# Searching the top-k thresholds of a hybrid decoder block: four of seven query blocks on ScalarE with 16-bit integer keys, three on VectorE

## The chip, the cores and the metric

The program runs on one core of one Trainium2 chip. The metric is the device time of one execution in microseconds (us); of several runs the median is taken. The engines go by the names of the profile: PE is TensorE's matrix product (PEld its weight load), DVE is VectorE, ACT is ScalarE, POOL is GpSimd, SP is SyncE, which issues most transfers. Each engine works through its own queue strictly in order, and waits for others by semaphores.

## The reference

A decoder block for 1024 tokens behind 16 meta tokens. Two attentions run on the same normed input: a sliding window with sinks, and a sparse attention whose keys an indexer chooses. Only the indexer's choice matters here:

```python
score = jnp.einsum('bqhs,bqh->bqs', jax.nn.relu(logits).astype(jnp.float32), wi.astype(jnp.float32))
admissible = (kpos[None, :] <= qpos[:, None]) & (kpos[None, :] >= PAD)
score = jnp.where(admissible[None], score, -jnp.inf)
_, sel = lax.top_k(score, topk)          # topk = 256 of up to 1040 keys
valid = (sel <= qpos[None, :, None]) & (sel >= PAD)
```

Each query keeps its 256 best keys, the earlier key first where scores are equal, and the sparse attention is a softmax over those alone. Behind the two attentions come gates, the output projection and a SwiGLU.

## The kernel before, in words

The tokens lie in eight blocks of 128 queries. Block j sees `width(j)` = 16 + 128(j+1) keys (144 for block 0, 1040 for block 7). Block 0 needs no choice; for blocks 1 to 7 the kernel finds, for each of the 128 queries of a block (one per partition), the exact 32-bit threshold that 256 scores reach, and turns it into an additive mask of 0 and -1e30 (`self.mask[j]`).

The search (`select_topk`) is by bits. The upper 16 bits of the scores lie as bf16 in `self.high[j]`. For each of 16 bits `count` compares all keys of a block with the trial threshold and adds up the hits in the same instruction (L772, one instruction for each block, and a short one that reads the accumulator); two small steps on [128 x 7] numbers set or clear the bit for all seven blocks at once (L779, L780). One more count closes the upper half. Then POOL takes the lower 16 bits of the scores (L789), DVE keeps those whose upper half equals the threshold's (L790), and 16 more bits are counted in them, with three small steps each (L794 to L796). At the end the mask is built: compare with the full threshold (L772 again, L808), a running count of equal scores for the ties (L809, a scan), two combinations (L810, L811), the scale to 0 and -1e30 (L812), and the causal edge (POOL, L534).

What runs beside the search: `proj_tokens`, `window_inputs`, `latents` and `sparse_inputs` project the tokens on PE (L189); ACT takes the products out of PSUM (L561 to L564, L601, L603) and rounds the weights to a high part (L183), POOL computes the low part (L184). `latents` needs DVE in the middle of it: L215 to L220 compute a reciprocal square root in some twelve small steps (`rlat`), L582 scales the rows by it (`lraw`), PE transposes them (L194), ACT and DVE split them into `ck` and `qn` (L125, L131). Then comes the window attention (`window_setup`, 16 calls of `window_block`): a DVE clear (L147) of the values `va`, the keys `ka` (load, ACT L685, DVE L686), products `s<-ka` (L189), a DVE step (L718) on each, and so on. Products of the gates (`gps`, `gt`, `w_hi`, `w_lo`; L835, L836) are spread between all this by a list of marks, so that PE has something to do.

What sets the order: the framework schedules every engine's queue ahead of time with a timeline of its own, and where two instructions could both go, the one that was written first goes first. `select_topk` is written ahead of `proj_tokens` and all that follows, so on DVE the steps of the search go first, and other work enters where the search has to wait for a result of its own.

Of the kernel before, what the change touches and what calls it, by code (L numbers as in the profile page):

```python
# [18 lines left out]
P = 128  # L19
# [3 lines left out]
NB = T // P  # L23
# [49 lines left out]
def width(j):  # L73
    return NM + P * (j + 1)
# [25 lines left out]
class Program:  # L100
# [18 lines left out]
    def split(self, ps, hi, lo, scale=None, lo_pool=False):  # L119
# [4 lines left out]
        else:  # L124
            nc.scalar.activation(hi, ps, AF.Copy, scale=scale)  # L125
        if lo_pool:
# [6 lines left out]
    def spread(self, ps, hi, lo, scale):  # L133
# [5 lines left out]
        for e in range(2):  # L139
            own, other = slice(64 * e, 64 * e + 64), slice(64 - 64 * e, 128 - 64 * e)  # L140
            nc.scalar.activation(hv[own, :, e, :], ps[own], AF.Copy, scale=scale)
            nc.vector.scalar_tensor_tensor(lv[:64, :, e, :], ps[own], scale, hv[own, :, e, :].bitcast(F32),
# [309 lines left out]
    def indexer(self, ip):  # L452
# [56 lines left out]
        for j in range(1, NB):  # L509
            W = width(j)  # L510
            iqt = iqts[j]
# [245 lines left out]

    def select_topk(self, ap):

        nc = self.nc  # L760
        n = NB - 1
        nc.vector.memset(self.mask[0], 0.0)
        self.causal(self.mask[0][:, NM:], P, 0, NEG)
        small = ap.tile([P, 7 * n], F32, name="small")
        cnt, thr, d, need, low, sign, base = [small[:, n * i:n * i + n] for i in range(7)]
        tb, d = thr.bitcast(I32), d.bitcast(I32)
        nc.vector.memset(thr, 0.0)
        rows = range(1, NB)

        def count(op, at, src, out=cnt):  # L770
            for j in rows:
                nc.vector.tensor_scalar(self.mask[j], src[j], at[:, j - 1:j], None, op0=op, op1=ALU.add, accum_out=out[:, j - 1:j])  # L772

        for k in range(31, 15, -1):
            count(ALU.is_ge, thr, self.high)
            nc.vector.tensor_scalar(d, cnt, float(TOPK), -65536.0 if k == 31 else float(1 << k), op0=ALU.is_lt, op1=ALU.mult)  # L779
            nc.vector.scalar_tensor_tensor(tb, d, 1 << (k - 1) if k > 16 else 0, tb, op0=ALU.bitwise_xor, op1=ALU.bitwise_xor)  # L780
        nc.vector.tensor_scalar(base, tb, 0.0, 65535.0, op0=ALU.is_lt, op1=ALU.mult)
        nc.vector.tensor_scalar(sign, base, -2.0 / 65535, 1.0, op0=ALU.mult, op1=ALU.add)
        count(ALU.is_gt, thr, self.high, need)
        nc.vector.tensor_scalar(need, need, -1.0, float(TOPK), op0=ALU.mult, op1=ALU.add)
        lows = [None] + [h.bitcast(U16) for h in self.high[1:]]
        for j in rows:
            half = self.mask[j].bitcast(U16)
            src = self.scores[j].bitcast(U16).rearrange("p (n e) -> p n e", e=2)[:, :, 0]
            nc.gpsimd.tensor_scalar(half, src, sign[:, j - 1:j], base[:, j - 1:j], op0=ALU.mult, op1=ALU.add)  # L789
            nc.vector.scalar_tensor_tensor(lows[j], self.high[j], thr[:, j - 1:j], half, op0=ALU.is_equal, op1=ALU.mult)  # L790
        nc.vector.memset(low, 32768.0)
        for k in range(15, -1, -1):
            count(ALU.is_ge, low, lows)
            nc.vector.tensor_sub(cnt, cnt, need)  # L794
            nc.vector.tensor_scalar(cnt, cnt, 0.0, 0.5 if k else 1.0, op0=ALU.is_ge, op1=ALU.subtract)
            nc.vector.scalar_tensor_tensor(low, cnt, float(1 << k), low, op0=ALU.mult, op1=ALU.add)  # L796
        nc.vector.tensor_mul(low, low, sign)
        nc.vector.tensor_add(d, low, base)
        nc.vector.scalar_tensor_tensor(tb, d, 0, tb, op0=ALU.bitwise_xor, op1=ALU.bitwise_xor)
        count(ALU.is_gt, thr, self.scores)  # L800
        nc.vector.tensor_scalar(cnt, cnt, -1.0, float(TOPK), op0=ALU.mult, op1=ALU.add)
        for j in rows:
            W = width(j)
            s = self.scores[j]
            t = thr[:, j - 1:j]
            eq = self.mask[j]
            rank = self.high[j].bitcast(mybir.dt.int16)
            nc.vector.tensor_scalar(eq[:, :W], s, t, None, op0=ALU.is_equal)  # L808
            nc.vector.tensor_tensor_scan(rank[:, :W], eq[:, :W], eq[:, :W], 0.0, op0=ALU.add, op1=ALU.max)  # L809
            nc.vector.scalar_tensor_tensor(eq[:, :W], rank[:, :W], cnt[:, j - 1:j], eq[:, :W], op0=ALU.is_le, op1=ALU.mult)  # L810
            nc.vector.scalar_tensor_tensor(eq[:, :W], s, t, eq[:, :W], op0=ALU.is_gt, op1=ALU.add)  # L811
            nc.vector.tensor_scalar(self.mask[j], eq[:, :W], -1.0, -NEG, op0=ALU.add, op1=ALU.mult)  # L812
            self.causal(self.mask[j][:, W - P:], P, 0, NEG)

    def gates(self, *cuts):
        behind, n, marks = list(self.tensor_insts), (32 - LATE) * KC * 3, [None] * GSP[0]
# [654 lines left out]
```

## Time and profile before

| | |
|---|---|
| median of 3 runs | 1561.67 us (1555.85 to 1562.71) |
| the profiled execution, device time | 1559.75 us |
| its span, first to last instruction | 1558.0 us |
| PE busy | 1394.5 us (90% of the span) |
| DVE busy | 1132.3 us (73%) |
| ACT busy | 709.2 us (46%) |
| POOL busy | 822.9 us (53%) |
| mean granted TensorE clock | 0.957 of full speed |

The profiled execution lies 1.9 us under the median. Its span leaves 1.75 us of the device time outside. Busy shares are averages over stages that have different limits; which wait counts has to be read stage by stage. Durations of single instructions overlap a little at their ends, so where many follow each other the distance from start to start is the price.

### The profile page before, as it was taken

The page shows a single profiled execution, that of the slowest core. Times are in us where ns is not written, and L with a number is a line of the kernel's source. Part 1 is how long each engine was busy: PE and PEld are TensorE (multiplying, and loading weights), DVE is VectorE, ACT ScalarE, POOL GpSimd, SP SyncE. Part 2 cuts the span into 40 slices and gives each one's busy share as a digit, 9 for nine tenths or more (in the row PEclk, how much of TensorE's full clock was granted, in tenths as well). Part 3 has the DMA queues.
Part 4 walks back from the last instruction along what each step waited for, and adds up shares of the span by engine and source line. Part 5 has one row for each costly group of instructions (what it writes and reads, how often), then busy time and mean ns, then how long its engine had stood idle before and what let it go on. Part 6 is the DMA issues. An engine that isn't in the chain of part 4 may idle for free.

```text
span 1558.0 us, 21095 instructions
## 1 busy us (share of the span) xinstructions
PE 1394.5 (90%) x6847; PEld 1155.7 (74%) x6847; DVE 1132.3 (73%) x2205; ACT 709.2 (46%) x1479; POOL 822.9 (53%) x768
## 2 busy tenths in 40 slices
PE   4999966295699899999999789999999999999997
PEld 4989955184577687889777568888888888878876
DVE  6268999999877678778498995444444446698576
ACT  5344311142288677777334553333333334433463
POOL 4232304113566555675588385555555557596575
PEclk9999998697899899999999899999999999999999
DMA  6420212044333755434861113332333338822332
GB/s 201 129 75 28 77 53 68 28 162 124 106 108 102 186 129 171 146 112 144 277 222 54 54 34 116 108 108 102 103 103 103 104 104 289 324 75 95 119 119 108
DMA packets 148036, 189.77 MB, mean 122 GB/s; under 512 B 11331, under 2 KB 95126, under 8 KB 147670
## 3 DMA queue, kind: packets, MB, share of 16 engines
q1 hardware_dynamic: 147568, 188.28, 37.5%
q8 instruction: 54, 0.88, 0.2%
q14 instruction: 56, 0.46, 0.1%
q10 hardware_dynamic: 198, 0.14, 0.0%
q0 software_dynamic: 160, 0.01, 0.0%
HBM read 133.49 MB, written 58.03 MB: 123 GB/s over the span
## 4 chain that ended last, share of the span: by engine, by line
PE 56%; DVE 27%; DMA 6%; POOL 4%; issue 4%; ACT 2%; SPq 1%; POOLq 0%; DVEq 0%; ACTq 0%
PE ps L189 22%; PE s L189 17%; DVE mask L772 12%; PE gps L189 8%; PE pv L970 2%; PE s L928 2%; PE tp L959 1%; DMA kraw<-bk_dram 1%; PE tp L194 1%; PE pv L189 1%; POOL yhl L1353 1%; POOL y L1432 1%; DVE high L809 1%; DVE fhl L1353 1%; DMA wd<-in_w_ffn_down 1%
## 5 line engine op out<-in xcount | busy, mean ns | idle before, releaser
L1282 POOL TENSOR_TENSOR fhl<-fs,fhl 128x512 fp32r<-128x512 f32 x88 | 121.3, 1400 | 99.1 <-ACT fhl L1281 99.1
L772 DVE TENSOR_SCALAR_CACHE_REDUCE mask<-high,small 128x272 bf16<-128x272 bf16 (+9 forms) x165 | 153.3, 972 | 3.6 <-POOL high L529 2.6
L1282 POOL TENSOR_TENSOR fhl<-fr,fhl 128x512 fp32r<-128x512 f32 x66 | 105.2, 1614 | 84.7 <-ACT fhl L1281 72.9
L184 POOL TENSOR_TENSOR w_lo<-w_raw,w_hi 128x512 fp32r<-128x512 f32 x60 | 82.4, 1375 | 114.3 <-ACT w_hi L183 99.8
L189 PE MATMUL s<-ht,fhl 128*128 128x512 f32 x384 | 123.3, 396 | 2.4 <-ACT fhl L1281 2.0
L1353 POOL TENSOR_TENSOR yhl<-wd,yhl 128x512 fp32r<-128x512 f32 x66 | 96.1, 1461 | 54.4 <-ACT yhl L1352 54.3
L1353 DVE TENSOR_TENSOR fhl<-da,fhl 128x512 fp32r<-128x512 f32 x66 | 89.4, 1369 | 46.4 <-ACT fhl L1352 46.3
L189 PE MATMUL ps<-ht,fhl 128*128 128x512 f32 x320 | 101.1, 392 | 0.0
L189 PE MATMUL gps<-oh,w_hi 128*128 128x512 f32 x232 | 96.0, 414 | 4.6 <-ACT gt L835 4.5
L189 PE MATMUL s<-yhl,fhl 128*128 128x512 f32 x396 | 92.4, 391 | 2.5 <-POOL yhl L1353 2.3
L189 PE MATMUL gps<-ol,w_hi 128*128 128x512 f32 x232 | 94.0, 405 | 0.0
L189 PE MATMUL gps<-oh,w_lo 128*128 128x512 f32 x232 | 93.5, 403 | 0.0
L189 PE MATMUL ps<-yhl,fhl 128*128 128x512 f32 x396 | 92.1, 391 | 1.5 <-DVE fhl L1353 1.5
L189 PEld LDWEIGHTS s<-yhl,fhl 128*128 128x128 f32 x396 | 73.9, 188 | 20.2 <-POOL yhl L1353 4.3
L189 PE MATMUL s<-h,fhl 128*128 128x512 f32 x272 | 88.7, 397 | 0.0
L189 PEld LDWEIGHTS ps<-yhl,fhl 128*128 128x128 f32 x396 | 73.9, 188 | 18.9 <-DVE fhl L1353 3.1
L189 PEld LDWEIGHTS s<-ht,fhl 128*128 128x128 f32 x384 | 72.8, 190 | 20.0 <-ACT fhl L1281 2.9
L129 DVE TENSOR_TENSOR ptl<-tp,pth 128x512 fp32r<-128x512 f32 (+2 forms) x112 | 70.8, 646 | 22.7 <-ACT pth L123 22.3
L189 PE MATMUL ps<-h,fhl 128*128 128x512 f32 x256 | 82.4, 393 | 3.6 <-ACT h L1239 3.6
L1352 ACT CAST yhl<-wd 128x512 fp32r<-128x512 f32 x66 | 40.9, 620 | 94.6 <-PE ps L189 42.8
L189 PE MATMUL s<-lt,fhl 128*128 128x512 f32 x192 | 76.0, 396 | 1.6 <-DVE lt L1240 1.6
L1281 ACT CAST fhl<-fr 128x512 fp32r<-128x512 f32 x66 | 39.7, 619 | 74.4 <-issue 33.2
(456 smaller groups left out, 4245.7 us busy)
## 6 DMA issues: line engine op xcount, KB each, us to landing
fr<-in_w_ffn_gate SPq DMA_DIRECT2D x22, 512.0 KB, 3.8
fr<-in_w_ffn_up SPq DMA_DIRECT2D x22, 512.0 KB, 4.7
wd<-in_w_ffn_down SPq DMA_DIRECT2D x44, 256.0 KB, 5.3
da<-acts SPq DMA_DIRECT2D x44, 256.0 KB, 3.8
w_raw<-in_w_in SPq DMA_DIRECT2D x40, 256.0 KB, 3.2
act<-a SPq DMA_DIRECT2D x33, 256.0 KB, 2.0
da<-act SPq DMA_DIRECT2D x33, 256.0 KB, 3.0
acts<-s SPq DMA_DIRECT2D x33, 256.0 KB, 2.0
```

The costliest lines, as they stand in the source:

```text
L129: nc.vector.tensor_sub(lo, ps, hi.bitcast(F32))
L184: (nc.vector if lo_dve else nc.gpsimd).tensor_sub(t[1], t[2], t[0].bitcast(F32))
L189: mm = self.nc.tensor.matmul(*args, **kw)
L194: mm = self.nc.tensor.transpose(*args)
L772: nc.vector.tensor_scalar(self.mask[j], src[j], at[:, j - 1:j], None, op0=op, op1=ALU.add, accum_out=out[:, j - 1:j])
L809: nc.vector.tensor_tensor_scan(rank[:, :W], eq[:, :W], eq[:, :W], 0.0, op0=ALU.add, op1=ALU.max)
L928: nc.tensor.matmul(ps[:, :n], q[k][:, h, qc:qc + P], kb[:, h, at:at + n], start=k == 0, stop=k == 1)
L970: mm = nc.tensor.matmul(acc[:, e, :], v, t[k][:, 256 * i:256 * i + 256], start=r + i + k == 0, stop=False)
L1281: nc.scalar.copy(hi, a[name])
L1282: nc.gpsimd.tensor_sub(lo, a[name], hi.bitcast(F32))
L1352: nc.scalar.copy(hi, src)
L1353: (nc.gpsimd if pool else nc.vector).tensor_sub(lo, src, hi.bitcast(F32))
```

## The change

`DVE_ROWS = (6, 4, 1)` stay with VectorE and the algorithm of before (`search_dve`; the small steps now work on [128 x 3]). `ACT_ROWS = ((7, 2), (5, 3))` are two groups that ScalarE searches (`search_act`). Their upper halves become signed 16-bit integer keys (POOL L849, DVE L851). A trial is one ACTIVATE of Sign over all keys of a block with a bias for each query and the sum of the signs in the accumulator (L857); POOL compares the sum for each block (L865) and makes the next bias for the group (L866). 16 bits on the keys, one closing count, the low halves (POOL and DVE, `low_halves`), 16 bits on those, and six small DVE steps that put the threshold together. The three searches are written as generators and called in turn, a bit each. The masks are built as before, except that the scale to 0 and -1e30 moves from DVE to POOL.

The diff, cut:

```diff
+DVE_ROWS = (6, 4, 1)
+ACT_ROWS = ((7, 2), (5, 3))
...
+        searches = [self.search_act(ap, f"g{i}", g, thr[:, places[g[0]]:places[g[0]] + len(g)]) for i, g in enumerate(ACT_ROWS)]
+        searches.append(self.search_dve(ap, DVE_ROWS, thr[:, :nd]))
+        while searches:
+            searches = [s for s in searches if next(s, None) is not None]
+        for j in range(1, NB):
+            nc.vector.tensor_scalar(self.mask[j], self.scores[j], col(thr, j), None, op0=ALU.is_gt, op1=ALU.add, accum_out=col(cnt, j))
...
-            nc.vector.tensor_scalar(self.mask[j], eq[:, :W], -1.0, -NEG, op0=ALU.add, op1=ALU.mult)
+            nc.gpsimd.tensor_scalar(self.mask[j], eq[:, :W], -1.0, -NEG, op0=ALU.add, op1=ALU.mult)
...
+    def low_halves(self, j, equal, sign, base):
...
+        nc.gpsimd.tensor_scalar(half, src, sign, base, op0=ALU.mult, op1=ALU.add)
+        nc.vector.scalar_tensor_tensor(self.lows[j], *equal, half, op0=ALU.is_equal, op1=ALU.mult)
...
+    def search_act(self, ap, tag, rows, thr):
...
+        for i, j in enumerate(rows):
+            key, t = keys[j], t = self.high[j].bitcast(I16), self.mask[j].bitcast(I16)
+            g.tensor_scalar(t, key, 0.0, 32767.0, op0=ALU.is_lt, op1=ALU.mult)
+            k32 = key.bitcast(I32)
+            nc.vector.tensor_tensor(k32, k32, t.bitcast(I32), op=ALU.bitwise_xor)
...
+        def count(src, at, out, scale=1.0):
+            for i, j in enumerate(rows):
+                nc.scalar.activation(self.mask[j], src[j], AF.Sign, bias=at[:, i:i + 1], scale=scale, accum_out=out[:, i:i + 1])
...
+            for k in range(15, -1, -1):
+                count(src, b, acc, 2.0 ** -k)
+                for i in range(n):
+                    o = slice(i, i + 1)
+                    g.tensor_scalar(c[:, o], acc[:, o], bar[:, o], b[:, o], op0=ALU.is_ge, op1=ALU.subtract)
+                g.tensor_scalar(b, c, -2.0 if k else -1.0, 1.0, op0=ALU.mult, op1=ALU.add)
+                yield k
...
+        nc.vector.tensor_add(l, T1, base)
+        nc.vector.tensor_scalar(h, T0, 1.0, 0.0, op0=ALU.mult, op1=ALU.add)
+        nc.vector.tensor_scalar(t, T0, 0.0, 32767.0, op0=ALU.is_lt, op1=ALU.mult)
+        nc.vector.tensor_tensor(h, h, t, op=ALU.bitwise_xor)
+        nc.vector.tensor_scalar(h, h, 16, None, op0=ALU.logical_shift_left)
+        nc.vector.tensor_tensor(thr.bitcast(I32), h, l, op=ALU.bitwise_or)
```

In the changed kernel all later lines have other numbers: L561 of before is L565, L582 is L586, L147 is L151, L183 and L184 are L187 and L188, L685 and L686 are L689 and L690, L718 is L722, L835 is L914. The numbers of PE's products do not change, 6847 in all, but their order does.

The first place is ACT's queue while the second part of `proj_tokens` is taken out of PSUM (`junk`, `lraw`, `vraw` are the three readings of one product). Before:

```order
L561 ACTIVATE junk,ssq<-ps 128x128
L562 COPY lraw<-ps 128x128
L564 COPY vraw<-ps 128x128
L561 ACTIVATE junk,ssq<-s 128x128
L562 COPY lraw<-s 128x128
L564 COPY vraw<-s 128x128
```

In the changed kernel, same place (`mask_151` and `mask_146` are blocks 7 and 2, `mask_149` and `mask_147` blocks 5 and 3):

```order
L565 ACTIVATE junk,ssq<-s 128x128
L566 COPY lraw<-s 128x128
L568 COPY vraw<-s 128x128
L857 ACTIVATE mask_149,smallg_1221<-high,smallg_1221 128x784
L857 ACTIVATE mask_147,smallg_1221<-sc_203,smallg_1221 128x528
L565 ACTIVATE junk,ssq<-ps 128x128
L566 COPY lraw<-ps 128x128
L568 COPY vraw<-ps 128x128
```

One group's pass, two ACTIVATEs, now stands between two readings of products.

POOL's queue at the same place in the changed kernel (before, POOL had the weights' low parts and the gates alone there):

```order
L865 TENSOR_SCALAR smallg_1221<-smallg_1221 128x1 x2
L866 TENSOR_SCALAR smallg_1221<-smallg_1221 128x2
L188 TENSOR_TENSOR w_lo<-w_raw,w_hi 128x512
L865 TENSOR_SCALAR smallg_1208<-smallg_1208 128x1 x2
L866 TENSOR_SCALAR smallg_1208<-smallg_1208 128x2
L915 TENSOR_SCALAR gt<-gt 128x512
```

The three small steps behind each pass share the queue with the weights' low parts and the gates.

The second place is DVE's queue where `lraw` is scaled. Before, just behind the closing count of the upper half (17 of 33 counts are done):

```order
L782 TENSOR_SCALAR small_1206<-small_1206 128x7
L772 TENSOR_SCALAR mask4_148,small_1206<-high_204,small_1206 128x656
L772 TENSOR_SCALAR mask5_149,small_1206<-high_204,small_1206 128x784
L772 TENSOR_SCALAR mask6_150,small_1206<-high_204,small_1206 128x912
L772 TENSOR_SCALAR mask7_151,small_1206<-high_204,small_1206 128x1040
L582 TENSOR_SCALAR lraw_1607<-lraw_1607,rlat_y_2119 16x128
```

In the changed kernel, behind the last bit of DVE's own search:

```order
L833 TENSOR_SCALAR smalld_1234<-smalld_1234 128x3
L223 SCALAR_TENSOR_TENSOR rlat_a_2359<-rlat_a_2359,ssq_1849 128x18
L834 SCALAR_TENSOR_TENSOR smalld_1234<-smalld_1234 128x3
L224 SCALAR_TENSOR_TENSOR rlat_y_2358<-rlat_a_2359,rlat_y_2358 128x18
L836 TENSOR_TENSOR smalld_1234<-smalld_1234 128x3
L586 TENSOR_SCALAR lraw_1846<-lraw_1846,rlat_y_2358 16x128
```

`lraw` moved from the middle of the search of seven blocks to the end of the search of three.

The third place is the end of the masks and the start of the window attention on DVE. Before, the clears stood between the scans:

```order
L809 SCALAR_TENSOR_TENSOR high_204<-mask4_148 128x656
L147 CAST va_2831<-zero_284 128x256
L151 CAST qlo0_2852<-zero_284 64x1024
L151 CAST qlo1_2853<-zero_284 64x1024
L147 CAST pth_2900<-zero_284 128x512
L147 CAST ptl_2901<-zero_284 128x512
L809 SCALAR_TENSOR_TENSOR high_204<-mask5_149 128x784
```

In the changed kernel they stand behind the last mask step:

```order
L791 SCALAR_TENSOR_TENSOR mask2_146<-sc1_203,small_1206,mask2_146 128x400
L791 SCALAR_TENSOR_TENSOR mask7_151<-sc0_202,small_1206,mask7_151 128x1040
L151 CAST va_3070<-zero_284 128x256
L155 CAST qlo0_3091<-zero_284 64x1024
L155 CAST qlo1_3092<-zero_284 64x1024
L151 CAST pth_3139<-zero_284 128x512
L151 CAST ptl_3140<-zero_284 128x512
L690 TENSOR_TENSOR ka0_3079<-kraw_3081,ka0_3079 64x1040
```

The clear of `va`, which starts the loads of the window attention's keys, now waits for the masks of blocks 7 and 2.

## Rows read from the trace of the kernel before

**Rows 1.** Busy time by stage. Columns: the stretch in us from the span's start, its length, then busy us and count of PE, PEld, DVE, ACT, POOL, then the granted TensorE clock, the share of the DMA engines and GB/s.

```profile
137.00:222.00 85.00, 84.98 (x589) 78.13 (x588) 83.17 (x211) 23.59 (x80) 15.34 (x13) 1.00 0.21 60
222.00:244.00 22.00, 0.00 (x0) 0.00 (x0) 22.00 (x64) 0.00 (x0) 4.90 (x7) 0.62 0.00 0
244.00:274.60 30.60, 28.59 (x117) 21.83 (x117) 30.36 (x69) 7.70 (x15) 14.36 (x9) 0.94 0.29 95
274.60:304.10 29.50, 0.07 (x2) 0.02 (x1) 28.95 (x76) 1.12 (x3) 3.07 (x3) 0.56 0.07 18
304.10:366.00 61.90, 61.90 (x277) 51.23 (x278) 60.73 (x159) 22.59 (x42) 10.17 (x10) 0.96 0.53 172
366.00:421.00 55.00, 28.09 (x104) 21.86 (x104) 52.52 (x63) 10.30 (x14) 24.91 (x20) 0.75 0.27 74
421.00:539.00 118.00, 103.64 (x535) 83.54 (x534) 84.94 (x257) 90.79 (x247) 72.17 (x102) 0.97 0.45 125
```

**Rows 2.** Who PE waited for between 137 and 430 us: us in total, times, the longest.

```profile
PE tp L194 <- DVE qn L131: 29.4, 1, 29.4
PE tp L194 <- DVE lraw L582: 22.2, 1, 22.2
PE s L189 <- DVE ka L686: 10.9, 1, 10.9
```

**Rows 3.** DVE in order of time, one bit of the upper half (start us, us): counts of some of the seven blocks (272 keys are block 1, 400 block 2, 784 block 5, 912 block 6, 1040 block 7), and the next bit's first count.

```profile
139.36 0.50 DVE L772 TENSOR_SCALAR_CACHE_REDUCE mask<-high,small 128x272 bf16<-128x272 bf16 x1
139.78 0.63 DVE L772 TENSOR_SCALAR_CACHE_REDUCE mask<-sc,small 128x400 bf16<-128x400 bf16 x1
...
141.02 0.89 DVE L772 TENSOR_SCALAR_CACHE_REDUCE mask<-high,small 128x656 bf16<-128x656 bf16 x1
...
141.84 1.02 DVE L772 TENSOR_SCALAR_CACHE_REDUCE mask<-high,small 128x784 bf16<-128x784 bf16 x1
...
142.79 1.16 DVE L772 TENSOR_SCALAR_CACHE_REDUCE mask<-high,small 128x912 bf16<-128x912 bf16 x1
...
143.87 1.29 DVE L772 TENSOR_SCALAR_CACHE_REDUCE mask<-high,small 128x1040 bf16<-128x1040 bf16 x1
...
145.62 0.50 DVE L772 TENSOR_SCALAR_CACHE_REDUCE mask<-high,small 128x272 bf16<-128x272 bf16 x1
```

**Rows 4.** DVE in order of time: the first small step of two lower bits that follow each other.

```profile
264.35 0.17 DVE L794 TENSOR_TENSOR small<-small 128x7 f32<-128x7 f32 x1
...
270.82 0.16 DVE L794 TENSOR_TENSOR small<-small 128x7 f32<-128x7 f32 x1
```

**Rows 5.** DVE in order of time: where block 7's scores begin, the two small steps of one bit while POOL computed low parts of weights, and the scaling of `lraw` (ten instructions).

```profile
129.83 0.97 DVE L524 TENSOR_SCALAR sc<-relu,iw 128x1040 f32<-128x1040 f32 x1 [0.98 <-ACT relu L520]
...
157.71 1.04 DVE L779 TENSOR_SCALAR small<-small 128x7 int32<-128x7 f32 x1
158.78 1.22 DVE L780 SCALAR_TENSOR_TENSOR small<-small 128x7 int32<-128x7 int32 x1
...
242.95 5.20 DVE L582 TENSOR_SCALAR lraw<-lraw,rlat_y 16x128 f32<-16x128 f32 x10
```

**Rows 6.** PE in order of time: two products of 512 columns that follow each other.

```profile
215.64 0.39 PE L189 MATMUL s<-oh,wa_hi 128*128 128x512 f32 x1
215.86 0.39 PE L189 MATMUL s<-ol,wa_hi 128*128 128x512 f32 x1
```

**Rows 7.** ACT by line and shape: busy us, mean ns of one. An Exp over the keys of a block with a bias for each query and a sum in the accumulator, late in the kernel.

```profile
L935 ACT ACTIVATE pb<-pb,st 128x1040 f32<-128x1040 f32 x8 | 9.4, 1172 | 3.3 <-DVE st L932 3.3
L935 ACT ACTIVATE pb<-pb,st 128x784 f32<-128x784 f32 x8 | 7.6, 955 | 1.6 <-DVE st L932 1.4
L935 ACT ACTIVATE pb<-pb,st 128x528 f32<-128x528 f32 x8 | 5.9, 739 | 0.3 <-DVE st L932 0.3
L935 ACT ACTIVATE pb<-pb,st 128x400 f32<-128x400 f32 x8 | 5.1, 634 | 0.9 <-DVE st L932 0.9
```

**Rows 8.** POOL's smallest arithmetic step, from the listing of one source line: ns (min/median/max), first and last start, shape.

```profile
L936 POOL TENSOR_SCALAR pmq<-pb x64: 196/203/1167, 543.2 to 727.3; 128x16 f32<-128x16 f32 x64
```

**Rows 9.** POOL by line and shape (busy us, mean ns): low parts of the weights.

```profile
L184 POOL TENSOR_TENSOR wa_lo<-wa_raw,wa_hi 128x512 fp32r<-128x512 f32 x22 | 31.5, 1440 | 69.8 <-ACT wa_hi L183 69.6
```

**Rows 10.** The chain that ended last, in order of time, at the end of the masks (start us, us).

```profile
370.82 5.80 DVE mask L772 x14
...
391.02 10.06 DVE high L809 x3
401.08 5.87 DVE mask L810 x7
...
408.02 4.55 DVE mask L811 x6
412.57 0.03 issue
412.60 1.25 DVE ka L686
413.85 0.04 issue
413.89 1.13 PE s L189 x4
```

**Rows 11.** ACT in order of time: its part of the window attention's first keys, with the wait ahead of it.

```profile
390.19 1.06 ACT L685 CAST ka<-kraw 128x1040 fp32r<-128x1040 f32 x1 [2.43 <-DMA kraw<-wk_dram]
```

More of the change, by code (lines that the diff above doesn't have):

```diff
@@ L12 @@
 U16 = mybir.dt.uint16
+I16 = mybir.dt.int16
 AF = mybir.ActivationFunctionType
@@ L763, in select_topk @@
         self.causal(self.mask[0][:, NM:], P, 0, NEG)
-        small = ap.tile([P, 7 * n], F32, name="small")
-        cnt, thr, d, need, low, sign, base = [small[:, n * i:n * i + n] for i in range(7)]
+        small = ap.tile([P, 2 * n], F32, name="small")
+        thr, cnt = small[:, :n], small[:, n:]
+        nc.vector.memset(thr, 0.0)
+        self.lows = [None] + [h.bitcast(U16) for h in self.high[1:]]
+        places = {j: i for i, j in enumerate((*DVE_ROWS, *[j for g in ACT_ROWS for j in g]))}
@@ new lines, in select_topk @@
+        col = lambda t, j: t[:, places[j]:places[j] + 1]
+        nd = len(DVE_ROWS)
+        searches = [self.search_act(ap, f"g{i}", g, thr[:, places[g[0]]:places[g[0]] + len(g)]) for i, g in enumerate(ACT_ROWS)]
[4 more added lines that the diff above has]
+            nc.vector.tensor_scalar(self.mask[j], self.scores[j], col(thr, j), None, op0=ALU.is_gt, op1=ALU.add, accum_out=col(cnt, j))
@@ new lines, in select_topk @@
+        nc.vector.tensor_scalar(cnt, cnt, -1.0, float(TOPK), op0=ALU.mult, op1=ALU.add)
+        for j in range(1, NB):
+            W = width(j)
+            s, t = self.scores[j], col(thr, j)
+            eq = self.mask[j]
+            rank = self.high[j].bitcast(I16)
+            nc.vector.tensor_scalar(eq[:, :W], s, t, None, op0=ALU.is_equal)
+            nc.vector.tensor_tensor_scan(rank[:, :W], eq[:, :W], eq[:, :W], 0.0, op0=ALU.add, op1=ALU.max)
+            nc.vector.scalar_tensor_tensor(eq[:, :W], rank[:, :W], col(cnt, j), eq[:, :W], op0=ALU.is_le, op1=ALU.mult)
+            nc.vector.scalar_tensor_tensor(eq[:, :W], s, t, eq[:, :W], op0=ALU.is_gt, op1=ALU.add)
+            nc.gpsimd.tensor_scalar(self.mask[j], eq[:, :W], -1.0, -NEG, op0=ALU.add, op1=ALU.mult)
+            self.causal(self.mask[j][:, W - P:], P, 0, NEG)
@@ new lines, in low_halves, with search_dve @@
+    def low_halves(self, j, equal, sign, base):
+        nc = self.nc
+        half = self.mask[j].bitcast(U16)
+        src = self.scores[j].bitcast(U16).rearrange("p (n e) -> p n e", e=2)[:, :, 0]
+        nc.gpsimd.tensor_scalar(half, src, sign, base, op0=ALU.mult, op1=ALU.add)
+        nc.vector.scalar_tensor_tensor(self.lows[j], *equal, half, op0=ALU.is_equal, op1=ALU.mult)
+    def search_dve(self, ap, rows, thr):
+        nc, n = self.nc, len(rows)
+        small = ap.tile([P, 6 * n], F32, name="smalld")
+        cnt, d, need, low, sign, base = [small[:, n * i:n * i + n] for i in range(6)]
@@ L766, in select_topk @@
         tb, d = thr.bitcast(I32), d.bitcast(I32)
-        nc.vector.memset(thr, 0.0)
-        rows = range(1, NB)
         def count(op, at, src, out=cnt):
-            for j in rows:
-                nc.vector.tensor_scalar(self.mask[j], src[j], at[:, j - 1:j], None, op0=op, op1=ALU.add, accum_out=out[:, j - 1:j])
+            for i, j in enumerate(rows):
+                nc.vector.tensor_scalar(self.mask[j], src[j], at[:, i:i + 1], None, op0=op, op1=ALU.add, accum_out=out[:, i:i + 1])
         for k in range(31, 15, -1):
@@ L784, in select_topk @@
         nc.vector.tensor_scalar(need, need, -1.0, float(TOPK), op0=ALU.mult, op1=ALU.add)
[L785 to L790, printed above, removed]
+        for i, j in enumerate(rows):
+            c = slice(i, i + 1)
+            self.low_halves(j, (self.high[j], thr[:, c]), sign[:, c], base[:, c])
         nc.vector.memset(low, 32768.0)
         for k in range(15, -1, -1):
-            count(ALU.is_ge, low, lows)
+            count(ALU.is_ge, low, self.lows)
             nc.vector.tensor_sub(cnt, cnt, need)
@@ L796, in select_topk @@
             nc.vector.scalar_tensor_tensor(low, cnt, float(1 << k), low, op0=ALU.mult, op1=ALU.add)
+            yield k
         nc.vector.tensor_mul(low, low, sign)
```

39 lines of the change are left out of this document (26 added, 13 removed).

## The prediction

> **What bounds the kernel now.** I read the busy times by stage first. Over the whole span PE is busy 90%, but in three stages it is not: 222 to 244 us, 274.6 to 304.1 and 366 to 421. There it is busy 0, 0.07 and 28.09 us, while DVE is full (22.00 of 22, 28.95 of 29.5, 52.52 of 55), and the granted clock is 0.62, 0.56 and 0.75 [rows 1]. Then I read whom PE waited for: 22.2 us for `lraw`, 29.4 for `qn`, 10.9 for the first `ka`, all three written by DVE [rows 2]. So from 130 to 414 us the search on DVE sets the time, and the projections of PE lie beside it, cut in pieces by single DVE steps that queue behind the search. The profiled execution (1559.75 us, 1.9 under the median) is my base. What counts is when the first product of the window attention starts, 413.89 us before: behind it stands the same work in nearly the same order, so I take a shift of that start as the shift of the end.
>
> **DVE's own search.** One bit of the upper half takes 6.26 us from start to start for seven blocks; of it block 1 takes 0.42, block 4 0.82 and block 6 1.08, and what no count holds is the 0.53 us between the end of block 7's count and the next bit (145.62 − 143.87 − 1.22, its slot) [rows 3]. Three blocks: 2.32 + 0.53 = 2.85 us a bit. A lower bit takes 6.47 us, 0.2 more, since it has one small step more [rows 4]: 3.04 with three blocks. From 129.8 us, where block 7's scores begin and take 5.2 us [rows 5]: 5.2, the rest of the first pass 1.6, 15 × 2.85 = 42.8, the flips of the integer keys 1.1, the closing count with base and sign 2.9, low halves 4 (an estimate, from three counts and a hand-over to POOL), 16 × 3.04 = 48.6, and some 2.8 for steps of the other searches and of `rlat`. That is 109 us, so `lraw` could be scaled at 239.
>
> DVE's small steps are dearer while POOL works: 1.04 and 1.22 us where the same kind takes 0.17 [rows 4, 5]. Now POOL has more to do, and DVE more small steps for each us. About ten of 32 bits met such a step before; at 0.9 us each I add 8 us. `lraw` at **247 us**, against 242.95 before [rows 5]: scarcely moved, though it now stands behind a whole search. PE gets to this wait earlier: 47 products fewer stand ahead of it, and two of 512 columns start 0.22 to 0.23 us apart [rows 6], so 10.7 of the 85 us [rows 1] go, and some 3 come from waits for ACT, whose passes stand between the readings of PSUM. PE is there at 213 to 217 and waits some 30 us (22.2 before).
>
> **PE from `lraw` to the first `ka`.** Nothing of the search on DVE is left there, so the wait for `qn` (29.4) goes, and the 47 products plus 22 from later stages, 69 in all, fill in. The path: before, PE was busy 28.59 + 61.90 + some 21 (of the 28.09 us of the last stage, what lay ahead of 413.89) = 111.6 us [rows 1]. Plus 69 × 0.228 = 15.7: 127 us at the clocks of before. At full clock the same 478 products and the small ones come to 117. That puts PE at the first `ka` between 247 + 117 = 364 and 374. I take 372, since a gap of 30 us stands ahead of it, and behind such gaps the stretch was granted 0.94 to 0.96, not 1 [rows 1].
>
> **ACT's search.** No row shows a Sign. The nearest is Exp with a bias for each query and a sum in the accumulator: 1172 ns for 1040 keys, 634 for 400, 955 for 784, 739 for 528 [rows 7]. From start to start I take 0.01 less: a pass of blocks 7 and 2 costs 1.78 us, one of 5 and 3 1.68. Bounds: DVE's own count of 1040 keys (1.29 us) above [rows 3], and half of Exp's price below; the Exp is nearest, being the same instruction with another function. One pass of each group hides what POOL does for the other: two steps of [128 x 1] and one of [128 x 2], at 0.2 us (POOL's smallest arithmetic step: median 203 ns, worst 1167) [rows 8], 0.6 us behind a pass of 1.7. What isn't hidden is when a low part of a weight, 1440 ns on POOL [rows 9], stands ahead. POOL is then taken about a third of the time; I take 0.3 us for each pass.
>
> ACT's order puts one eviction (`ck`, which needs PE's transposes of `lraw`) ahead of 14 passes of one group and 18 of the other, so until 248 us ACT can do the first halves only, and the rest comes after: 14 × 1.68 + 18 × 1.78 = 55.5 us, plus some 20 of evictions and roundings of weights (two thirds of the 7.70 + 1.12 + 22.59 us that ACT had from 244 to 366 [rows 1]), plus 32 × 0.3 = 10 us of hand-over: the searches end near **334 us**. Behind that come on DVE six small steps (2 us), the counts and compares of the last two blocks (3, of the 5.80 for seven [rows 10]), their scans (4 to 6; three long ones took 10.06), and seven and seven combinations (5.87, and 4.55 for six plus 1.3): 21 us in all, 355. The clear of `va` now comes behind these masks; it starts the loads of the keys, and from the clear to ACT's copy of the first `ka` lie 0.3 on DVE, 0.9 on ACT and POOL and 4.9 for the load, then 1.06 on ACT [rows 11] and 1.25 on DVE [rows 10]: 8.4 us, which before lay beside the scans. First product at 363.5 by this path.
>
> The scale of the masks leaves DVE and goes to POOL, some 2.5 us less on DVE and 6 more on POOL; the causal edge on POOL that follows it is not waited for until the sparse attention, so I put it at nothing. If that cover were gone, it would cost these 6 us.
>
> **The sum.** The later of the two paths: 372 (PE), 363.5 (ACT). 413.89 − 372 = 42 us: 1559.75 − 42 = **1518 us**, with 1502 to 1538 for PE at full clock with no waits (356) up to an exposure of 1.1 us a pass (392).
>
> **The rule that speaks against this.** ACT's Exp takes 1172 ns for 1040 keys, DVE's count 1.29 us for the same keys [rows 3, 7]: the two engines stand level. The Trainium skill ("ScalarE: Activation LUTs", section "Rules for kernel authors") says to keep simple arithmetic off ScalarE, since VectorE is up to about 3 times faster for each element in bf16 with one source. By that rule a pass of both groups would be 11.1 us (3 × the counts of 1.29, 1.02, 0.76 and 0.63) and not 3.5; the searches would end 110 us later. The rows bear it out only for plain copies; a count with a sum is not such.
>
> **The rivals.**
>
> *POOL's answer is exposed, break-even.* The chain of one group is pass, wait, three POOL steps, wait, pass. If the exposure is x us a pass and not 0.3, the first product comes at 352.5 + 32x, and at x = 1.92 at 413.89: no gain (1557). For it: the queue of POOL holds 1440 ns steps [rows 9]; against: these have gaps of their own, and the other group covers 1.7 us.
>
> *The same mechanism, slower than before.* Place: POOL between two passes on ACT. Price: three steps at 1167 ns (the worst of the small ones [rows 8]), which happen when DVE works beside it, plus 0.4 behind a low part, less what is covered: x = 3.6. First product at 468, 1559.75 + 54 = **1613**. It decides from x = 1.92 on. For it: POOL and DVE lengthen each other's steps [rows 5]; against: the median is 203 ns [rows 8].
>
> *DVE's small steps wait for POOL in every bit.* 1.9 us (1.04 + 1.22 less two of 0.17 [rows 4, 5]) × 32 = 61: `lraw` at 300 and the first product at 417 to 427: 1563 to 1573. For it: POOL has three more steps for every pass; against: those are short.
>
> *Better than forecast.* No exposure, full clock: 239 + 117 = 356, and 22 products fewer (5 us) behind it: 1497.
>
> *ACT at a third of DVE's pace:* first product at 473, 1619 us. It is what the rule of the Trainium skill cited above would make; the trace speaks against it (1172 ns against 1.29 us).
>
> **How the numbers follow.** Forecast 0.66; better 0.09; break-even 0.10; slower through POOL 0.08; DVE behind POOL 0.06; ACT slow 0.01. About half of the break-even case would still show a gain over 0.5% (7.8 us, about what a measurement of this kernel can tell from no change), and half of the DVE case would be a loss over it. Faster: 0.66 + 0.09 + 0.05 = 0.80; same: 0.05 + 0.03 = 0.08; slower: 0.08 + 0.03 + 0.01 = 0.12. The range goes from 1492, a little under the better case, to 1555, where the break-even case begins; it leaves out about 2 in 10.
>
> **What would show it.** `lraw` scaled near 247 us with some 30 us of idle PE ahead of it and a low clock there; no wait for `qn`; ACT's Sign at 1.17 us for 1040 keys, the last one near 334; POOL's three steps at 0.2 us each, with a wait of ACT for POOL of some 10 us in all; the first product of the window attention near 372. I am wrong on DVE if `lraw` is later than 260, on ACT if the last Sign comes after 345, and on the carry-through if the start moves by 42 us and the end by much less, say because the window attention then waits for a load or for ACT.

## The result, and the profile after

The changed kernel takes **1517.02 us** (median of four runs, 1515.01 to 1521.55) against 1562.01 us (1555.85 to 1562.71) before: a ratio of 0.9725, 95% interval 0.9692 to 0.9758. That is 45 us less; the forecast was a time of 1518 us. The profiled execution has a span of 1514.8 us, 43.2 us less than the 1558.0 before. So the total was right. Its terms were not all right: the first product of the window attention starts 31.3 us earlier, not 42, and the rest is gained behind it. One later run of 3488 us (four blocks on VectorE, the second time) was disturbed, and neither its time nor its profile is used.

The busy times of the changed kernel in the stretches of before (columns as in [rows 1]):

```profile
137.00:222.00 85.00, 71.32 (x493) 66.12 (x492) 80.46 (x223) 62.89 (x179) 47.08 (x100) 0.90 0.14 39
222.00:244.00 22.00, 11.30 (x57) 9.34 (x56) 21.54 (x77) 7.57 (x18) 7.62 (x14) 0.80 0.16 47
244.00:274.60 30.60, 26.97 (x109) 21.56 (x109) 12.77 (x25) 22.84 (x53) 25.64 (x45) 0.89 0.20 62
274.60:304.10 29.50, 28.64 (x128) 23.03 (x127) 2.82 (x4) 29.18 (x66) 19.32 (x43) 0.97 0.32 99
304.10:366.00 61.90, 59.57 (x267) 48.45 (x266) 36.05 (x50) 43.42 (x92) 37.94 (x65) 1.00 0.55 180
```

PE's idle stretch from 274.6 us is filled (28.64 us, 0.07 before), the one from 222 us half filled. DVE is full until 244 us and then has room: 2.82 of 29.5 us. But PE gets less done between 137 and 222 us: 493 products in 71.32 busy us, where it had 589 in 84.98. Who waited for whom between 130 and 430 us (in total, times, longest; PE's part answers to [rows 2]):

```profile
ACT mask L857 <- POOL smallg L866: 28.1, 11, 11.3
ACT mask L857 <- DVE smalld L832: 14.1, 1, 14.1
PE tp L198 <- DVE lraw L586: 10.7, 1, 10.7
PE s L193 <- POOL wa_lo L188: 7.8, 2, 7.3
PE s L193 <- DVE ka L690: 7.6, 1, 7.6
PE s L193 <- ACT wa_hi L187: 7.4, 2, 3.8
```

The wait for `qn` (29.4 us) is gone, those for `lraw` and `ka` are shorter, and there are new ones, for the halves of weights that ACT and POOL make beside the search.

DVE in order of time, block 6's count in two upper and in two lower bits that follow each other, and the end of `rlat` (answers to [rows 3 to 5]):

```profile
137.27 1.16 DVE L815 TENSOR_SCALAR_CACHE_REDUCE mask<-high,small 128x912 bf16<-128x912 bf16 x1
140.11 1.16 DVE L815 TENSOR_SCALAR_CACHE_REDUCE mask<-high,small 128x912 bf16<-128x912 bf16 x1
...
227.78 1.16 DVE L815 TENSOR_SCALAR_CACHE_REDUCE mask<-high,smalld 128x912 bf16<-128x912 uint16 x1
...
230.83 1.16 DVE L815 TENSOR_SCALAR_CACHE_REDUCE mask<-high,smalld 128x912 bf16<-128x912 uint16 x1
...
233.15 0.17 DVE L571 TENSOR_SCALAR ssq<-ssq 128x9 f32<-128x9 f32 x1
...
241.51 0.18 DVE L224 SCALAR_TENSOR_TENSOR rlat_y<-rlat_a,rlat_y 128x18 f32<-128x18 f32 x1
...
241.80 0.54 DVE L586 TENSOR_SCALAR lraw<-lraw,rlat_y 16x128 f32<-16x128 f32 x2
```

A bit is 2.84 and 3.05 us long; 2.85 and 3.04 were worked out. The small steps of `rlat` begin at 233.15 us (L571), where DVE's order has them, and end 8.5 us later with the search, one between two steps of the search each. ACT had the last sum of squares that they need at 217.6 us.

ACT by line and shape (busy us, mean ns of one; answers to [rows 7]) and, from the listings of two source lines, POOL's steps behind a pass (ns min/median/max; [rows 8]):

```profile
L857 ACT ACTIVATE mask<-high,smallg 128x1040 bf16<-128x1040 int16 x17 | 20.0, 1177 | 6.0 <-POOL smallg L866 3.8 <-DVE high L851 2.2
L857 ACT ACTIVATE mask<-high,smallg 128x784 bf16<-128x784 int16 x17 | 16.4, 966 | 15.4 <-POOL smallg L866 14.9 <-DVE high L851 0.5
L857 ACT ACTIVATE mask<-sc,smallg 128x528 bf16<-128x528 int16 x17 | 12.6, 741 | 0.0
L857 ACT ACTIVATE mask<-sc,smallg 128x400 bf16<-128x400 int16 x17 | 10.8, 636 | 0.4 <-DVE sc L851 0.4
```

```profile
L865 POOL TENSOR_SCALAR smallg<-smallg x128: 357/364/5652, 111.1 to 336.8; 128x1 f32<-128x1 f32 x128
L866 POOL TENSOR_SCALAR smallg<-smallg x64: 185/191/1213, 132.2 to 337.3; 128x2 f32<-128x2 f32 x64
```

A Sign costs what an Exp of the same shape cost. A comparison on POOL takes 364 ns, not 203; three steps are 0.92 us, not 0.6.

The chain of waits from the masks to the first product (start us, us; answers to [rows 10, 11]). DVE's clear of `va` was at 359.96 us, behind the last mask step:

```profile
366.38 1.28 POOL w_lo L188
367.66 1.90 POOL bt_a L544
...
370.12 0.61 POOL gt L915
370.74 1.51 POOL va L676
...
373.08 0.51 POOL bt_a L545
...
374.96 0.45 POOL va L676
...
375.96 4.18 DMA kraw<-wk_dram
...
380.22 1.07 ACT ka L689
...
381.31 1.25 DVE ka L690
...
382.61 1.12 PE s L193 x4
```

From the clear to the product are 22.6 us where 8.4 were forecast: POOL first finished seven scales and seven causal edges of the masks (until 365.2 us), then stood with low parts, a bias mask and gates ahead of `va`. The clear itself held nothing up here: ACT's copy of the values waited for their load, until 363.05 us, when the clear had long been done.

### The profile page after: what moved, and what is told of

It is laid out like the page before. It is cut to its first block, busy times and chain, and to the rows that moved or that the text cites. A ratio compares the mean times of both kernels' runs of the same rounds, so it can differ in the third digit from the quotient of the medians.

```text
span 1514.8 us, 21375 instructions
## 1 busy us (share of the span) xinstructions
PE 1398.1 (92%) x6847; PEld 1160.4 (77%) x6847; DVE 1009.9 (67%) x1950; ACT 817.0 (54%) x1743; POOL 914.7 (60%) x995
## 4 chain that ended last, share of the span: by engine, by line
PE 60%; DVE 15%; POOL 7%; issue 7%; ACT 6%; DMA 6%; SPq 1%; POOLq 0%; ACTq 0%; DVEq 0%
PE ps L193 24%; PE s L193 20%; PE gps L193 8%; DVE mask L815 4%; ACT mask L857 2%; PE pv L1049 2%; PE s L1007 2%; PE tp L1038 2%; DMA kraw<-bk_dram 1%; DMA ga<-gate_dram 1%; POOL yhl L1432 1%; POOL y L1511 1%; PE tp L198 1%; PE pv L193 1%; DVE fhl L1432 1%
## 5 line engine op out<-in xcount | busy, mean ns | idle before, releaser
L188 POOL TENSOR_TENSOR w_lo<-w_raw,w_hi 128x512 fp32r<-128x512 f32 x60 | 82.4, 1375 | 90.5 <-ACT w_hi L187 76.3
L857 ACT ACTIVATE mask<-high,smallg 128x784 bf16<-128x784 uint16 (+3 forms) x66 | 70.4, 1067 | 45.9 <-POOL smallg L866 28.1
L865 POOL TENSOR_SCALAR smallg<-smallg 128x1 f32<-128x1 f32 x128 | 58.8, 462 | 59.8 <-ACT mask L857 59.3
L1431 ACT CAST yhl<-wd 128x512 fp32r<-128x512 f32 x66 | 41.0, 621 | 95.0 <-PE ps L193 43.2
```

The costliest lines, as they stand in the source:

```text
L188: (nc.vector if lo_dve else nc.gpsimd).tensor_sub(t[1], t[2], t[0].bitcast(F32))
L857: nc.scalar.activation(self.mask[j], src[j], AF.Sign, bias=at[:, i:i + 1], scale=scale, accum_out=out[:, i:i + 1])
L865: g.tensor_scalar(c[:, o], acc[:, o], bar[:, o], b[:, o], op0=ALU.is_ge, op1=ALU.subtract)
L1431: nc.scalar.copy(hi, src)
```

## The experiments

The theory I went in with (theory 1): the work that leaves DVE is the gain; the start of the window attention is then set by ACT's searches, the masks on DVE, and POOL's queue behind them, and PE only waits at the end. Rivals: PE's own path from `lraw` sets that start; the gain comes from something that the change does beside the search; the hand-over between ACT and POOL is exposed. First products and spans below are those of the profiled execution, ratios those of timed runs.

**The base.** The changed kernel, unedited.

> The changed kernel itself, once more, as the base for the runs beside it: 1515 to 1519 us, the first product of the window attention at 382.6 us, 31 us earlier than before, with 7 to 8 us of idle PE ahead of it.

Measured: 1521.23 us, ratio 0.9746 (0.9722 to 0.9771), 2 us over the range that was expected; first product at 385.93 behind 7.7 us of idle PE, span 1520.1. Two series of one kernel thus lie 4 us apart, and their profiles 3 us at the start and 5 at the end. What differs by less than that is not told apart below.

**POOL's part of the values on DVE.**

```diff
-            nc.gpsimd.tensor_sub(va[:n, bs, :, 1, :], raw[:n, bs], va[:n, bs, :, 0, :].bitcast(F32))
+            nc.vector.tensor_sub(va[:n, bs, :, 1, :], raw[:n, bs], va[:n, bs, :, 0, :].bitcast(F32))
```

> The low part of the values is computed on DVE, which is idle there, and not on POOL behind the masks. Theory 1 (the start of the window attention is set by ACT's searches, the masks and POOL's queue behind them; PE only waits): the load of the keys starts some 8 us earlier, the first product comes when PE is free, at 375, and the time falls by 6 to 8 us to about 1510. Theory 2 (PE's path from lraw sets the start, the 7.6 us of idle PE are filled by other products anyway): no change, 1515 to 1519.

Measured: 1520.39 us, ratio 0.9743 (0.972 to 0.9766): no change beside the base. The first product came at 380.73, 5.2 us earlier than in the base and 5.7 later than theory 1 said, and the span is 2.6 us shorter. The chain of waits of this kernel shows why it was not more:

```profile
372.51 0.64 POOL gt L915
...
373.16 0.34 SPq L916
...
373.60 0.48 SPq L660
374.12 4.14 DMA kraw<-wk_dram
```

The values no longer need POOL, but the load of the keys (L660) stands on SP's queue behind the store of a gate (L916), and that gate is computed on POOL (L915) behind the masks. The wait went from one edge of POOL's queue to another. Theory 1 holds for the place (POOL's queue), not for the size. The time is theory 2's "no change", but not for its reason: the start did move.

**The scale of the masks back on DVE.** This undoes one part of the change.

```diff
-            nc.gpsimd.tensor_scalar(self.mask[j], eq[:, :W], -1.0, -NEG, op0=ALU.add, op1=ALU.mult)
+            nc.vector.tensor_scalar(self.mask[j], eq[:, :W], -1.0, -NEG, op0=ALU.add, op1=ALU.mult)
```

> One part undone: the masks' scale to 0 and -1e30 is on DVE again. Theory 1: DVE has 2.5 us more, POOL loses seven steps between the masks and the values; the first product comes near 377, the time near 1512. Theory 2: DVE's 2.5 us more are all that is seen, 1517 to 1520.

Measured: 1523.07 us, ratio 0.9762 (0.9738 to 0.9786); first product at 380.26, 5.7 us before the base; span 1518.3. The time lies over both forecasts. The start moved as theory 1 said, the time did not fall: of a start five microseconds earlier no more than 1.8 us are left in the span here, and 2.6 in the run before, which is inside what two profiles of one kernel differ by. Moving the scale to POOL neither helped nor hurt by an amount that can be measured.

**POOL's comparison twice.**

```diff
-                    g.tensor_scalar(c[:, o], acc[:, o], bar[:, o], b[:, o], op0=ALU.is_ge, op1=ALU.subtract)
+                    for _ in range(2):
+                        g.tensor_scalar(c[:, o], acc[:, o], bar[:, o], b[:, o], op0=ALU.is_ge, op1=ALU.subtract)
```

> POOL's comparison behind each pass is issued twice with the same result: two more steps of 0.36 us in each of 64 hand-overs. Theory 1 (the other group's pass covers the hand-over except where one group is alone or POOL is held up by a low part, some 11 waits): the searches end 6 to 10 us later, the time is 1523 to 1528. Rival (the hand-over is exposed in every pass of a group): 32 x 0.73 = 23 us, 1540. Rival (all covered): 1517.

Measured: 1528.88 us, ratio 0.9797 (0.9776 to 0.9817), 7.7 us over the base; first product at 387.20. By the time this is theory 1, a little over its upper end. By the trace it is nearer to the rival: the last Sign starts at 355.3 us, 18.2 later than the base's 337.1, which is 0.57 of the added 0.73 us in each of 32 passes. So the other group's pass covers less of the hand-over than I thought. The time can't weigh this, since two more things changed behind the searches. DVE's clear of `va` stands at 350.0 us, ahead of the last masks, and the last steps of the masks run behind the first keys. And one small step of the masks took 7.77 us, where it takes 0.16 in the changed kernel (DVE in order of time):

```profile
364.63 7.77 DVE L782 TENSOR_SCALAR small<-small 128x7 f32<-128x7 f32 x1
```

POOL worked from 362.08 to 372.37 us without a pause. How much of the 7.7 us in the time is the hand-over stays open.

**All seven blocks on VectorE, by the new code.**

```diff
-DVE_ROWS = (6, 4, 1)
-ACT_ROWS = ((7, 2), (5, 3))
+DVE_ROWS = (7, 6, 5, 4, 3, 2, 1)
+ACT_ROWS = ()
```

> All seven blocks are searched on VectorE by the changed kernel's code: what is left of the change is the searches as generators, the other order of the blocks and the masks' scale on POOL. Theory 1 (the work that leaves DVE is what gains): as the kernel before, 1555 to 1562 us. Rival (the moved scale or the new order of writing gains by itself): 1545 or less.

Measured: 1559.3 us, ratio 1.0005 (0.9986 to 1.0023). Theory 1: the new order of writing and the moved scale bring nothing by themselves. The first product of the profiled execution came at 407.03, 6.9 us earlier than before. That execution, 1554.31 us, is the lowest of ten and its span is 5.5 us shorter than before; the median shows nothing of it.

**Only PE's wait for `lraw`.** In the kernel before, the search is written behind the latents:

```diff
-        self.select_topk(tk)
         with self.pool("lt") as lp:
             self.proj_tokens(lp)
             self.window_inputs(lp)
             self.latents(lp)
+            self.select_topk(tk)
             self.sparse_inputs(lp)
```

> The kernel before, with one thing changed: the latents' steps on DVE are written ahead of the search, so that DVE takes them first and PE does not wait 22 us for lraw. Theory 1 (the length of DVE's search and masks sets the start of the window attention, 413.9 us; PE's waits are only how PE spends that time): no change, 1555 to 1563. Rival (PE's waits for lraw and qn are the loss and the gain of the change is that they go): 22 us or more faster, 1540 or less.

Measured: 1556.17 us, ratio 0.9983 (0.9969 to 0.9997). Who PE waited for, in the same stretch as above:

```profile
PE tp L194 <- DVE qn L131: 25.3, 1, 25.3
PE s L189 <- POOL wa_lo L184: 15.4, 1, 15.4
PE ps L189 <- ACT w_hi L183: 14.4, 1, 14.4
PE tp L194 <- DVE lraw L582: 10.6, 1, 10.6
```

Twelve microseconds of the wait for `lraw` go and a new wait for a weight's low part, 15.4, takes their place; the first product comes at 412.50 (413.89). The waits for `lraw` and `qn` lost 15.7 of their 51.6 us and the start moved by 1.4, so for as much as the edit took away, the gain is not in the waits themselves: they show where PE is idle, and the start goes with DVE's work. The rest of the two waits stood on.

**Another split, both ways.**

```diff
-DVE_ROWS = (6, 4, 1)
-ACT_ROWS = ((7, 2), (5, 3))
+DVE_ROWS = (6, 4, 3, 1)
+ACT_ROWS = ((7, 2), (5,))
```

> Block 3 is moved from ScalarE to VectorE (6, 4, 3, 1 on VectorE; 7, 2 and 5 on ScalarE). Theory 1 (ACT's searches and what follows them set the start, DVE has room): the searches on ACT end some 30 us earlier, the first product waits for PE alone and comes at 366 to 372 us, the time is 1506 to 1512. Rival (DVE is still the bound): 32 x 0.69 = 22 us later for DVE, 1530 or more.

Measured: 1507.69 us, ratio 0.9671 (0.9649 to 0.9693), as theory 1 said and clear of the base. The last Sign starts at 309.6 us; the first product comes at 369.0 and PE waits for no key any more:

```profile
368.77 0.39 PE L193 MATMUL gps<-ol,w_hi 128*128 128x512 f32 x1
368.99 0.23 PE L193 MATMUL s<-ka,qhi 128*128 128x144 f32 x1
```

With three blocks on VectorE, then, ACT was the later of the two searches; one more block on DVE costs nothing there.

```diff
-DVE_ROWS = (6, 4, 1)
-ACT_ROWS = ((7, 2), (5, 3))
+DVE_ROWS = (6, 1)
+ACT_ROWS = ((7, 2), (5, 4, 3))
```

> Block 4 is moved from VectorE to ScalarE (6, 1 on VectorE; 7, 2 and 5, 4, 3 on ScalarE). Theory 1: 33 passes of 656 keys at some 1.08 us with the sum's reading, 36 us more on ACT, of which 20 to 28 show at the start of the window attention: 1537 to 1545. Rival (DVE is still the bound): faster, 1510 or less.

Measured: 1524.75 us, ratio 0.9784 (0.9763 to 0.9806). That is 3.5 us over the base and not clear of it. The rival (faster) is out, but theory 1 said 16 us or more. 36 us of passes were added, and the last Sign starts at 351.1, only 14 us after the base's. A group of three blocks fills what had been waits:

```profile
ACT mask L857 <- POOL smallg L866: 11.0, 8, 4.6
ACT mask L857 <- POOL smallg L881: 3.7, 1, 3.7
```

In the changed kernel ACT waited 28.1 us for L866 on POOL and 14.1 for DVE's search; here it is 11.0 for L866, 3.7 for L881, and none for DVE's search. And DVE's clear again comes ahead of the last masks, so that the first product is not late (380.36), but DVE's first step on it is (386.73), with masks between. One compare of 400 keys for the masks (L788) took 4.93 us here, where it took 0.42 in the changed kernel; this is in the time too.

**Where ACT's longest wait comes from.** In the kernel with four blocks on VectorE, POOL and ACT in order of time:

```profile
197.24 4.88 POOL L801 TENSOR_SCALAR mask<-sc,smalld 128x912 uint16<-128x912 uint16 x4 [15.72 <-DVE smalld L823]
202.09 0.19 POOL L866 TENSOR_SCALAR smallg<-smallg 128x1 f32<-128x1 f32 x1
```

```profile
202.31 0.95 ACT L857 ACTIVATE mask<-high,smallg 128x784 bf16<-128x784 int16 x1 [16.11 <-POOL smallg L866]
```

POOL's part of the lower halves (L801) waits for DVE's closing count, and ACT's answer (L866) stands behind it. The changed kernel has the same: 11.13 us on POOL, 11.28 on ACT, and PE's 7.3 for `wa_lo` behind that. The edit takes DVE's own blocks off POOL: `low_halves` gets an engine, which `search_dve` gives as VectorE.

```diff
-        nc.gpsimd.tensor_scalar(half, src, sign, base, op0=ALU.mult, op1=ALU.add)
+        (eng or nc.gpsimd).tensor_scalar(half, src, sign, base, op0=ALU.mult, op1=ALU.add)
```

> Four blocks on VectorE once more, as the base for the two runs beside it: 1505 to 1510 us.

Measured: four runs of 1504.36 to 1512.77 us, ratio 0.9683 (0.9659 to 0.9707).

> Four blocks on VectorE, and their lower halves are taken on DVE and not on POOL, so that POOL does not wait for DVE's closing count with ACT's comparisons behind that wait (15.7 us on POOL, 16.1 on ACT, 8.2 on PE with four blocks). Theory 1 (that wait stalls ACT, whose evictions and roundings PE needs): PE's 8 us go, the first product comes near 361 us, 1500 to 1503. Rival (DVE's three to four us more delay lraw by as much, and the stall is made up on ACT before PE needs it): 1507 to 1511.

Measured: 1507.8 us, ratio 0.9663 (0.9644 to 0.9682): no change beside the run above; first product at 367.91, 1.1 us earlier than in the first profile with four blocks. By the time this is the rival, but its reason is not what the trace shows: `lraw` was scaled at 236.9 us, 1.8 earlier and not later, and in place of the stall behind POOL (31.7 us on ACT in all, now 7.6) ACT waits 28.8 us for DVE's own lower halves (L802).

> The changed kernel with the lower halves of VectorE's own three blocks on DVE. Theory 1: ACT's wait of 11.3 us and PE's of 7.3 behind POOL's wait go, ACT's searches end some 8 us earlier: 1509 to 1514. Rival: no change, 1516 to 1522.

Measured: 1511.95 us, ratio 0.9695 (0.967 to 0.972); first product at 373.98, 12 us before the base's. The intervals of this and of the base (0.9722 to 0.9771) just part, but that of the changed kernel's first series (0.9692 to 0.9758) overlaps it: a gain is not shown. The time lies where theory 1 put it, and so does the last Sign, 7.7 us before the base's. But the stall did not go, it changed its name. ACT's waits in this kernel:

```profile
ACT mask L857 <- DVE high L802: 22.9, 1, 22.9
ACT mask L857 <- POOL smallg L866: 6.4, 6, 2.3
```

Now ACT waits for DVE to put its lower halves together (L802), which stands behind the search on DVE, and PE waits 17.4 us for a high part of a weight on ACT where it had waited 7.3 for a low part on POOL.

## Why the prediction was right, step by step

- **What bounds the kernel**: right. One wait that [rows 2] does not show has the same cause: PE also waited 16.0 us for ACT's `w_hi`, until 386.13 us, and ACT had that step behind its copy of the values, which waited 16.65 us for DVE's clear.
- **DVE's own search**: right. Bits of 2.84 and 3.05 us; `lraw` scaled at 241.8 us, 5 before the forecast, since fewer of DVE's small steps met a busy POOL than I added, and it stands behind the whole search, as forecast: its sums were there at 217.6 us.
- **PE ahead of `lraw`**: wrong. Forecast were 213 to 217 us and a gap of 30; PE came at 231.4 and waited 10.7. From 130 us to there PE was busy 87.4 of 101.4 us, so some 14 us went into waits, where 3 had been put. ACT's and POOL's new work delays the halves of weights, above all in one stall, 11.1 us on POOL and 11.3 on ACT, which PE saw as 7.3.
- **PE from `lraw` on**: 127 us at most were forecast. From 242.13 to 375.03, where PE ran dry, are 132.9. The products were as worked out, 542 in 125.6 busy us; the 7.3 us of waits between them were not in the sum. PE was free at 375, not 372.
- **ACT's search**: right in its length, not in its hand-over. Sign at 1177, 966, 741 and 636 ns against 1172, 955, 739 and 634; the last pass ends at 336.7 us, 334 was forecast. From 247.8 us on, the listed waits for POOL are 1.35, 5.49, 0.32, 0.16 and 3.41 us, 10.7 in all, where 10 were put in. But the sign named in the prediction, some 10 us of waits for POOL in all, failed: they are 28.1, with 17.4 of them ahead of 247.8 us. And the 10.7 are right by luck. POOL's steps take 0.92 us, not 0.6, and the three long waits (10.25 us) are not those behind a low part that I had in mind alone: in each, POOL's two comparisons took 2.50, 5.99 and 3.61 us (from 245.00, 249.02 and 325.12) while DVE worked on `lraw`, the masks and the scans. With the doubled comparison four fifths of what was added showed at the searches' end.
- **The rule that spoke against the change**: by the Trainium skill ("ScalarE: Activation LUTs", section "Rules for kernel authors") simple arithmetic belongs on VectorE. Here a count of 1040 keys is 1.18 us on ACT and 1.29 on DVE [rows 3], so the measurement decides against the rule for a count with a sum. The prediction says that the rows bear the rule out for plain copies; no row of it shows that.
- **Masks to first product**: the step that failed. The masks ended at 360.0 us (355 by the forecast). Then I put the scale and the causal edge on POOL at nothing and the path from the clear to the product at 8.4 us; it is 22.6, since the values' low part and, in another way, the load of the keys stand in POOL's queue. So it was this path that came last, at 382.6 us where 363.5 was forecast for it, and not PE's (375, forecast 372); PE waited 7.6.
- **The start sets the end**: failed too, the other way. The start moved by 31.3 us, the end by 43.2. At the start itself, DVE's first step on a product came 7.1 us after the product before, and 0.7 after it now. DVE in order of time, before:

```profile
412.60 1.24 DVE L686 TENSOR_TENSOR ka<-kraw,ka 64x1040 fp32r<-64x1040 f32 x1
413.87 1.30 DVE L811 SCALAR_TENSOR_TENSOR mask<-sc,small,mask 128x1040 bf16<-128x1040 f32 x1
415.09 2.46 DVE L812 TENSOR_SCALAR mask<-mask 128x272 bf16<-128x272 bf16 x7
419.68 1.24 DVE L686 TENSOR_TENSOR ka<-kraw,ka 64x1040 fp32r<-64x1040 f32 x1 [2.13 <-ACT ka L685]
420.95 0.37 DVE L718 CUSTOM_DVE_ANT_0 pa<-s,bt_a,nsink 128x144 f32<-128x144 f32 x1
```

and in the changed kernel:

```profile
383.34 0.37 DVE L722 CUSTOM_DVE_ANT_0 pa<-s,bt_a,nsink 128x144 f32<-128x144 f32 x1 [0.79 <-PE s L193]
...
389.75 1.24 DVE L690 TENSOR_TENSOR ka<-kraw,ka 64x1040 fp32r<-64x1040 f32 x1
```

Masks stood in between (3.7 us), but they did not set the 7.1: behind them DVE still waited 2.13 us for ACT's copy of the second keys, whose step stood ahead of L718 in its queue. Now that step stands behind. In the run with all blocks on VectorE only one mask step (1.44 us) lies in between, and the distance is 6.9 all the same, behind a wait of 4.2 for the second keys. How far the 6.3 us reach the end is another matter. The span behind the first product in the profiled kernels, and how long PE was busy in it:

| masks on DVE | first product, us | span, us | span behind it, us | PE busy in it, us |
|---|---|---|---|---|
| behind the first keys: before; all on VectorE; latents first; two on VectorE | 413.9; 407.0; 412.5; 380.4 | 1558.0; 1552.5; 1554.1; 1523.4 | 1144.1; 1145.5; 1141.6; 1143.0 | 1081.5; 1081.5; 1079.1; 1076.0 |
| ahead of them: changed; base; values on DVE; scale on DVE; four on VectorE | 382.6; 385.9; 380.7; 380.3; 369.0 | 1514.8; 1520.1; 1517.5; 1518.3; 1503.6 | 1132.2; 1134.2; 1136.8; 1138.0; 1134.6 | 1075.2; 1070.9; 1079.6; 1074.8; 1071.4 |
| ahead, lower halves on DVE: four; three | 367.9; 374.0 | 1507.8; 1515.4 | 1139.9; 1141.4 | 1075.1; 1076.5 |

The means of the first and of the other two groups (1143.6 and 1136.7) are 6.9 us apart. Of that 4.7 lie in PE's busy time (means 1079.5 and 1074.8) and only 2.2 in its idle time, where the wait for DVE would have to show. The busy time fits the products that now come ahead of the start: the changed kernel has 24 fewer behind it by its trace (5110 against 5134), some 5.5 us at the 0.228 us of [rows 6], which I had counted as 5 for the better case alone. Of the 11.9 us that is about half. The rest is not settled: in the changed kernel's profile it is idle time of PE (57.0 us behind the start, 62.7 before), in the base, which is the same kernel, PE is idle as long as before (63.2) and its products are shorter. The run with POOL's comparison twice has 1139.2.

Three sums of the prediction do not come out of their own terms: ten small steps at 0.9 us are 9, not 8; an exposure of 1.1 us a pass gives 388 us by the prediction's formula, not 392; and at three times DVE's counts the 14 and 18 passes would be some 123 us longer, not 110. The first would move `lraw` by 1 us; the others stand in the range and in a rival.

So the forecast of 1518 was right in its mechanism, DVE's relief, which the run with all blocks on VectorE and the one with the latents first bear out. That its size came within a microsecond is luck: two errors cancel, a start 10.6 us too early, and 12 us behind it that I did not count.

## What to carry to other kernels

When work moves off the engine that bounds, ask next which queue of a helper engine it enters, and follow each of that queue's other customers, also through a third engine's queue (here a load behind a store behind a gate on POOL). A split between two engines is best set from both ends: here one block more on VectorE was worth another 10 us or so, and the best kernel of the study is that one, at 0.967 to 0.968 of before (0.966 with the lower halves on DVE, which is not told apart). Check whether work that you count to a stage ends before or behind the point from which you measure.

## What the hardware showed

- A Sign over 16-bit integers with a bias for each query and a sum costs the same as an Exp over f32 of the same shape (1177 and 1172 ns for 1040), and the reading of the sum, 192 ns in the median, hides: the next ACTIVATE started 1.15 us after the one before (238.41 to 239.56).
- On POOL a comparison of one number for each partition with two operands from memory takes 364 ns, and a multiply-add of two numbers by constants 191. Whether the operands make the difference was not tried.
- DVE's small steps, 0.16 us in the median, took up to 1.21 us in the changed kernel too, but in few of the 32 bits. A step of [128 x 7] took 7.77 us in the run with POOL's comparison twice, beside 10 us of unbroken work on POOL, and POOL's comparison of 364 ns took up to 5.65 us in the changed kernel, beside DVE's masks. What in the one held up the other, no run separates.
